# Casts of h in one chain in the down projection, and an earlier split of a sum of x in a SwiGLU block kernel

## The chip, the core and the metric

The kernel runs on one core of a Trainium2 chip. The metric is the device time of one execution in microseconds (us). Of several executions the median is given. A profiled execution is one more, from which the page and the trace come.

TensorE (PE in the profile) multiplies matrices into PSUM banks, VectorE (DVE) and ScalarE (ACT) do the elementwise work, GpSimd (POOL) and SyncE (SP) mostly issue DMAs here.

## The reference

One layer of an encoder on 512 tokens of width 1024, all in float32:

```python
for l in range(DEPTH):                                   # DEPTH = 1
    x = x + FFN_RES * _swiglu(_rmsnorm(x, norm_ffn1[l]), w_ffn1_gu[l], w_ffn1_down[l])
    h = _rmsnorm(x, norm_mix[l])
    ...                                                  # RG-LRU both ways, neighbourhood attention
    x = x + y @ w_out[l]
    x = x + FFN_RES * _swiglu(_rmsnorm(x, norm_ffn2[l]), w_ffn2_gu[l], w_ffn2_down[l])

def _swiglu(h, w_gu, w_down):
    g, u = jnp.split(h @ w_gu, 2, axis=-1)
    return (jax.nn.silu(g) * u) @ w_down
```

The change is in the two SwiGLU layers (FFN below). Their inner width, the features of h = silu(g) * u, is 2816: 22 tiles of 128 features.

## The kernel before

**Numbers.** Each float32 operand is split in a high part H, rounded to the type fp32r by a cast on ScalarE (L140, in `split`), and the remainder L, a subtraction on VectorE (L143) that needs the cast. A product is three matmuls: H by H, L by H, H by L. In names, `wh`/`wl` are the parts of weights, `xh`/`xl` of x, `hh`/`hl` of h, and `s1` to `s4` stand for sums of parts of x and both their parts.

**The products that give h.** Two of the 22 tiles of features are "plain". In the first FFN they are multiplied while x is loaded, kept token by token (`pre`), finished in `ready` (L508 to L511: silu, product, transpose, store to `hp`) and fetched back transposed. The other twenty are five units of four tiles, computed in `strassen` by a Strassen-Winograd scheme with seven products each, of the forms a11, a12, s1, s2, s4, s3, a22; a product is 24 matmuls (L317) into two banks. The sums of weights come from a DMA that accumulates on POOL's queue (`add`) and additions on VectorE (`sums`, L340). The sums of x are made once (`make_forms`: `raw` subtracts, `cut` splits); in the first unit of the first FFN `need("s1")` and so on puts the splits where the code stands. The last product of a unit, a22, is done within the next unit. Banks are copied out on ScalarE (`evict`, L348) or added on VectorE (`plus`, L353).

**From there to the down projection.** `gate` (L359) is silu on ScalarE, `put` multiplies by u (L370) and transposes 32x32 blocks (L372) on VectorE, and `flush` stores the four tiles of a unit to DRAM, `hd[u]`. `fetch(u)` reads a unit back with features on the partitions: two tiles `hT` of 256 tokens, each with four DMAs of POOL's queue. `cut(k)` splits the tile k of h from these two halves (casts of 256 tokens each) into `hh` and `hl` of 512 tokens, and `ahead(n)` calls it for all k below n and fetches a unit ahead.

**The down projection.** Its sum goes over k, the 22 tiles of h, into eight banks (m = 0 to 7, four of the pool `aux`, four of `acc`), so 24 matmuls for each k (`mm3`, L167 to L169). The first three k (`DFIRST`) are done in four groups of two banks:

```python
for g in range(4):
    outs = range(2 * g, 2 * g + 2)
    for m in outs:
        ps[m] = (aux_t, acc_t)[g % 2]()
    for k in first:
        for m in outs:
            put_in(m, k)
```

The last group's banks are those of the last unit's last product (`Z`); they come free when its silu has read them. `finish` is called between that product and its silu: it fetches the first unit, loads the weights of the first three k and splits h ahead, with high priority. `last_put` and `flush` of the last unit stand behind it.

**What sets the order.** A scheduler orders the instructions of each engine by their dependences, with those under `tc.high_priority()` first. `after(i, prev)` tells the scheduler to place `i` behind `prev`; it adds no semaphore, so it binds on the chip only through the order within a queue. `hold` does so behind the matmul marked last. Four pairs of buffers hold wh and wl, three the raw weights (`wraw`), four the `pair` tiles, five the tiles `PT`, which the loads of weights and `hT` share.

Of the kernel before, what the change touches and what calls it, by code (L numbers as in the profile page):

```python
# [86 lines left out]
def block_kernel(ctx: ExitStack, tc, a, out):  # L87
# [49 lines left out]

    def split(raw, H, L, act=True):
        if act:
            nc.scalar.activation(H, raw, AF.Copy)  # L140
        else:
            nc.vector.tensor_copy(H, raw)
        return nc.vector.tensor_tensor(L, raw, H.bitcast(F32), ALU.subtract)  # L143
# [96 lines left out]
    def after(i, prev, sync=False):  # L240

        i, prev = getattr(i, "ins", i), getattr(prev, "ins", prev)
        tc.add_manual_dep(i, prev.name, mybir.DependencyInfo(
            mybir.DependencyClass.Sync if sync else mybir.DependencyClass.NoSync, mybir.DependencyReason.DATA), reason="order")

    def hold(i):

        after(i, mark["mm"])
        return i
# [42 lines left out]
    def strassen(src, units, A, norm, hd, need, ready, finish, early):  # L292
# [58 lines left out]
        def plus(ts, pss):  # L351
            for t, ps in zip(ts, pss):
                nc.vector.tensor_tensor(t, t, ps, ALU.add)  # L353

        def gate(ts, th):
            ss = [big_t(n="s") for _ in ts]
            for tb, (s_, t) in enumerate(zip(ss, ts)):
                j = th * 2 + tb
                nc.scalar.activation(s_, t, AF.Silu, scale=rc[0][:, j : j + 1])  # L359
            return ss  # L360

        def flush(q=nc.sync):
            while out:
                to, t2 = out.pop(0)
                hold(q.dma_start(to, t2))

        def put(u, ss, ts, th):
            for tb, (s_, t) in enumerate(zip(ss, ts)):
                j = th * 2 + tb
                mark["h"] = nc.vector.scalar_tensor_tensor(t, t, rc[0][:, j : j + 1], s_, ALU.mult, ALU.mult)  # L370
                t2 = big_t(n="ht")
                nc.vector.transpose(  # L372
                    t2.rearrange("p (c f i) -> p f c i", c=NCB, i=32), t.rearrange("p (f c i) -> p f c i", c=NCB, i=32))
                out.append((hd[u][j], t2.rearrange("p (c x) -> p c x", c=NCB)))
# [1 line left out]
        def last_product(p, out_now=True):  # L376
            product(p["Z"], operands(p["a"]), "a22", False, True, out_now)

        def last_put(p):
            put(p["u"], gate(p["Z"], 1), p["u7"], 1)  # L380

        def begin(u):
            a_ = raws(u, 0, "pair", 4)
# [5 lines left out]
        for u in range(units):  # L389
            state_["u"] = u  # L390
            a_, Z, p1 = begun.pop(u) if u in begun else begin(u)
            c_ = raws(u, 2, "PT", 5)
            d_ = raws(u, 1, "PT", 5)
            b_ = raws(u, 3, "wraw", 3)
            if u == 0:
                add(u, a_, 1)
            if u == 0:
                rc.append(norm())
            if u == units - 1:
                need("plain")  # L400
            Y = [aux_t() for _ in range(2)]
            product(Y, operands(c_), "a12", True, True)
            if u == 0:
                need("s1")
            plus(p1, Y)
            if u > 0:
                s1 = gate(p1, 0)
            X = [aux_t() for _ in range(2)]
            w = operands(a_) if u == 0 else sums(a_, d_)
            product(X, w, "s1", True, False)  # L410
            add(u, d_, 3)
            p5 = evict(X, "p5")
            if u == 0 and early:
                begun[1] = begin(1)
            if prev:
                last_product(prev)
                last_put(prev)
            w = sums(a_, b_)
            if u == 0:
                need("s2")  # L420
            product(Z, w, "s2", False, False)
            add(u, a_, 2)
            u2 = evict(Z, "u2")
            if u == 0:
                need("s4")
            product(X, operands(b_), "s4", False, True)
            if u == 0:
                need("s3")
                ready(rc[0])
                s1 = gate(p1, 0)  # L430
            plus(u2, X)
            put(u, s1, u2, 0)
            product(Z, operands(d_), "s3", False, False, u < units - 1)
            plus(p5, Z)
            prev = dict(u=u, Z=Z, u7=p5, a=a_)
        last_product(prev, False)
        finish()
        last_put(prev)
        flush(nc.gpsimd)

    def ffn(wgu, ws, wd, xh, xl, forms, ssum, plain, res, emit_out, lead=None, end=None):
        units = (FT - plain) // 4
# [58 lines left out]
        def ready(rc):  # L501
            if not toks:
                return
            neg = tiny.tile([P, NCB], F32, tag="nrc", name=nm("nrc"))
            nc.vector.tensor_scalar(neg, rc, -1.0, None, ALU.mult)
            for tb, t in enumerate(toks):
                g, u = t[:, :half], t[:, half:]
                nc.scalar.activation(g, g, AF.Silu, scale=rc[:, tb : tb + 1])  # L508
                nc.vector.scalar_tensor_tensor(u, u, neg[:, tb : tb + 1], g, ALU.mult, ALU.mult)
                nc.vector.transpose(  # L510
                    g.rearrange("p (c f i) -> p f c i", c=NCB, i=32), u.rearrange("p (f c i) -> p f c i", c=NCB, i=32))  # L511
                hold(nc.sync.dma_start(hp[tb], g.rearrange("p (c x) -> p c x", c=NCB)))
# [3 lines left out]
             "a22": quarter(4, slice(half, T))}  # L516
        A.update({n: forms.S[n] for n in FORMS})

        turned, cuts = {}, {}

        def fetch(u):
            for th in range(2):
                t = big.tile([P, 8, NCB, 32], F32, tag="PT", bufs=5, name=nm("hT"))
                for c in range(NCB):
                    hold(nc.gpsimd.dma_start(
                        t[c * 32 : (c + 1) * 32].rearrange("p g f i -> p g (f i)"),
                        hd[u].rearrange("t (a i) c x -> c i (t a) x", a=NCB)[c][:, th * 8 : th * 8 + 8]))
                turned[u, th] = t
# [10 lines left out]
        def cut(k):  # L539
            cuts[k] = H, L = big_t(F32R, n="hh"), big_t(F32R, n="hl")  # L540
            if k < len(hs):
                split(hs[k], H, L)
                return
            u, f = (-1, k) if k < plain else divmod(k - plain, NCB)
            for th in range(2):
                c = slice(th * half, (th + 1) * half)
                v = lambda t: t[:, c].rearrange("p (g i) -> p g i", i=32)
                split(turned[u, th][:, :, f], v(H), v(L))

        def ahead(n):  # L550
            while len(cuts) < min(n, FT):
                k = len(cuts)
                if k >= plain and (k - plain) % NCB == 0:
                    u = (k - plain) // NCB
                    if u + 1 < units:
                        fetch(u + 1)
                cut(k)
# [5 lines left out]
        def finish():  # L563
            fetch(0)
            for k in first:
                ws_[k] = load_w(wd[k], 1024)
            with tc.high_priority():
                ahead(DFIRST + 3)

        strassen(ws, units, A, norm, hd, need, ready, finish, lead is not None)  # L570

# [704 lines left out]
```

## Time and profile before

| what | value |
|---|---|
| median of 3 runs | 1114.53 us (1113.95 to 1115.28) |
| the profiled execution | 1115.2 us |
| its span, first to last instruction | 1113.4 us |
| mean granted clock of TensorE | 0.99 |
| busy: TensorE, VectorE, ScalarE, POOL | 98, 69, 50, 18% |
| DMA | 198.17 MB, mean 178 GB/s |

In the rows of the profile that follow, a row of the order in time starts with the time from the span's start and the duration of one instruction in us, then the engine, the line of the kernel, the operation, the tiles written and read, and in brackets the wait just before and what ended it. A row of a stretch (A:B) has the length and then, for TensorE, its weight loads, VectorE, ScalarE and POOL, the busy us and the count; at its end the granted clock of TensorE (1.00 is full), the share of the DMA engines and GB/s. A row "out <- engine tile line" of the waits has us, count and the longest.

### The profile page before, as it was taken

The numbers are of one execution on the slowest core, as the hardware profiler recorded it, in microseconds if no ns is written. First come the engines' busy times: TensorE is split into PE (matmuls) and PEld (weight loads), VectorE is DVE, ScalarE is ACT, GpSimd is POOL, SyncE is SP. The second block draws the span as 40 slices with busy tenths as digits, with TensorE's granted clock in tenths as the row PEclk, the third lists the DMA queues.
The fourth block names the chain that finished last, engine by engine and source line by source line (L and its number), as shares of the span: only waits on it lengthen the run. The fifth ranks groups of instructions, "written<-read, shape, count | busy, mean of one in ns | idle before, by whom it ended". The sixth has DMA issues, their size and how long they took to land. (4 is left out here: it accounts for less than half of the span.)

```text
span 1113.4 us, 14401 instructions
## 1 busy us (share of the span) xinstructions
PE 1086.3 (98%) x5121; PEld 888.7 (80%) x5121; DVE 770.7 (69%) x1222; ACT 562.0 (50%) x866; POOL 197.7 (18%) x340
## 2 busy tenths in 40 slices
PE   9989999969999999999999999999999999989998
PEld 7778888858888777888877788888888888868887
DVE  6778788773325786899878896768677788772322
ACT  7745555542324668776645543356455555543310
POOL 0101012432000243132226322000001000331000
PEclk9999999999999999999999999999999999999999
DMA  9777766884332578384679566565476767774222
GB/s 362 167 193 191 204 177 161 213 250 128 101 102 90 165 209 232 121 234 119 198 222 257 163 220 219 154 229 176 99 194 180 193 195 170 200 245 140 95 76 76
DMA packets 67463, 198.17 MB, mean 178 GB/s; under 512 B 11072, under 2 KB 12864, under 8 KB 67392
## 3 DMA queue, kind: packets, MB, share of 16 engines
q1 hardware_dynamic: 46592, 136.60, 37.3%
q0 software_dynamic: 20512, 60.34, 24.2%
q8 instruction: 40, 0.66, 0.2%
q10 hardware_dynamic: 288, 0.32, 0.1%
q14 instruction: 31, 0.25, 0.1%
HBM read 162.06 MB, written 26.74 MB: 170 GB/s over the span
## 5 line engine op out<-in xcount | busy, mean ns | idle before, releaser
L143 DVE TENSOR_TENSOR wl<-wraw,wh 128x1024 fp32r<-128x1024 f32 (+2 forms) x147 | 168.7, 1149 | 173.4 <-ACT wh L140 170.5
L140 ACT ACTIVATE wh<-wraw 128x1024 fp32r<-128x1024 f32 (+2 forms) x135 | 134.5, 998 | 239.2 <-PE acc L168 163.7
L143 DVE TENSOR_TENSOR wl<-pair,wh 128x1024 fp32r<-128x1024 f32 x80 | 97.2, 1219 | 46.0 <-ACT wh L140 45.8
L140 ACT ACTIVATE wh<-pair 128x1024 fp32r<-128x1024 f32 x80 | 84.8, 1061 | 72.1 <-PE aux L317 51.9
L167 PE MATMUL acc<-xh,wh 128*128 128x512 f32 x288 | 113.9, 395 | 0.0
L169 PE MATMUL acc<-xh,wl 128*128 128x512 f32 x288 | 112.5, 391 | 0.0
L168 PE MATMUL acc<-xl,wh 128*128 128x512 f32 x288 | 112.5, 391 | 0.0
L317 PE MATMUL acc<-wh,s 128*128 128x512 f32 x320 | 99.1, 390 | 3.1 <-ACT s L140 2.0
L317 PE MATMUL aux<-wh,s 128*128 128x512 f32 x320 | 100.0, 393 | 2.1 <-ACT s L140 2.0
L167 PE MATMUL aux<-hh,wh 128*128 128x512 f32 (+1 forms) x179 | 70.4, 395 | 8.5 <-ACT hh L140 8.5
L168 PE MATMUL aux<-hl,wh 128*128 128x512 f32 (+1 forms) x179 | 70.7, 395 | 5.4 <-DVE hl L143 5.2
L892 PE MATMUL acc<-wh,xh 128*128 128x512 f32 x192 | 75.7, 394 | 0.0
L893 PE MATMUL acc<-wh,xl 128*128 128x512 f32 x192 | 74.8, 389 | 0.0
L894 PE MATMUL acc<-wl,xh 128*128 128x512 f32 x192 | 74.7, 389 | 0.0
L317 PEld LDWEIGHTS acc<-wh,s 128*128 128x128 f32 x320 | 60.0, 188 | 16.7 <-ACT s L140 2.4
L317 PEld LDWEIGHTS aux<-wh,s 128*128 128x128 f32 x320 | 60.7, 190 | 15.6 <-ACT s L140 2.4
L169 PE MATMUL aux<-hh,wl 128*128 128x512 f32 (+1 forms) x179 | 70.3, 393 | 0.0
L168 PE MATMUL acc<-hl,wh 128*128 128x512 f32 (+1 forms) x176 | 69.0, 392 | 0.0
L167 PE MATMUL acc<-hh,wh 128*128 128x512 f32 (+1 forms) x176 | 69.0, 393 | 0.0
L169 PE MATMUL acc<-hh,wl 128*128 128x512 f32 (+1 forms) x176 | 68.9, 391 | 0.0
L140 ACT ACTIVATE wh<-PT 128x1024 fp32r<-128x1024 f32 x40 | 42.3, 1060 | 44.9 <-PE acc L317 35.8
L167 PEld LDWEIGHTS acc<-xh,wh 128*128 128x128 f32 x288 | 54.1, 188 | 13.0 <-issue 2.3
(230 smaller groups left out, 2431.8 us busy)
## 6 DMA issues: line engine op xcount, KB each, us to landing
wraw<-wqkv SPq DMA_DIRECT2D x24, 512.0 KB, 4.3
wraw<-wg SPq DMA_DIRECT2D x24, 512.0 KB, 7.3
wraw<-w1d SPq DMA_DIRECT2D x22, 512.0 KB, 5.0
wraw<-w2d SPq DMA_DIRECT2D x22, 512.0 KB, 3.3
PT<-w1s SPq DMA_DIRECT2D x20, 512.0 KB, 6.1
hT<-hd POOLq DMA_DIRECT2D x80, 128.0 KB, 5.2
PT<-w2s SPq DMA_DIRECT2D x20, 512.0 KB, 4.0
hd<-ht SPq DMA_DIRECT2D x32, 256.0 KB, 6.1
```

Source lines behind the costliest of these rows:

```text
L140: nc.scalar.activation(H, raw, AF.Copy)
L143: return nc.vector.tensor_tensor(L, raw, H.bitcast(F32), ALU.subtract)
L167: nc.tensor.matmul(ps, wh, xh, start=first, stop=False, skip_group_check=skip)
L168: nc.tensor.matmul(ps, wh, xl, start=False, stop=False, skip_group_check=skip)
L169: mark["mm"] = nc.tensor.matmul(ps, wl, xh, start=False, stop=last, skip_group_check=skip)
L317: mark["mm"] = nc.tensor.matmul(pss[tb], x_[:, s], w_[:, c], start=first and k == 0 and x_ is xh_ and w_ is H, stop=k == 3 and w_ is L, sk ...
L892: nc.tensor.matmul(pss[j], xh[kk][:, tj], H[:, s], start=kk == 0, stop=False)
L893: nc.tensor.matmul(pss[j], xl[kk][:, tj], H[:, s], start=False, stop=False)
L894: mark["mm"] = nc.tensor.matmul(pss[j], xh[kk][:, tj], L[:, s], start=False, stop=kk == KT - 1)
```

## The change

In both down projections the casts of h are chained, each after the one that was made before it (`cast`), so that the two halves of a tile follow each other. `finish` splits four tiles ahead instead of six and without high priority, and fetches two units there (`fetch(1)` was called within `ahead`, at the first tile of the first unit, before; hence `k > plain`). The last silu (`gate` in `last_put`) is ordered behind the latest cast, which is that of the tile k = 3, and the last stores behind the last fetch. In the first unit of the first FFN `need("s2")` stands right behind `need("s1")` instead of behind the sums of weights of s2, and the first multiplication on a plain column block (L509 before, L512 after) is ordered behind the split of s4.

```diff
@@ -137,7 +137,7 @@
 
     def split(raw, H, L, act=True):
         if act:
-            nc.scalar.activation(H, raw, AF.Copy)
+            mark["H"] = nc.scalar.activation(H, raw, AF.Copy)
         else:
             nc.vector.tensor_copy(H, raw)
         return nc.vector.tensor_tensor(L, raw, H.bitcast(F32), ALU.subtract)
@@ -352,17 +352,21 @@
             for t, ps in zip(ts, pss):
                 nc.vector.tensor_tensor(t, t, ps, ALU.add)
 
-        def gate(ts, th):
+        def gate(ts, th, prev=None):
             ss = [big_t(n="s") for _ in ts]
             for tb, (s_, t) in enumerate(zip(ss, ts)):
                 j = th * 2 + tb
-                nc.scalar.activation(s_, t, AF.Silu, scale=rc[0][:, j : j + 1])
+                i = nc.scalar.activation(s_, t, AF.Silu, scale=rc[0][:, j : j + 1])
+                if prev is not None:
+                    after(i, prev)
             return ss
 
-        def flush(q=nc.sync):
+        def flush(q=nc.sync, prev=None):
             while out:
                 to, t2 = out.pop(0)
-                hold(q.dma_start(to, t2))
+                i = hold(q.dma_start(to, t2))
+                if prev is not None:
+                    after(i, prev)
 
         def put(u, ss, ts, th):
             for tb, (s_, t) in enumerate(zip(ss, ts)):
@@ -376,8 +380,8 @@
         def last_product(p, out_now=True):
             product(p["Z"], operands(p["a"]), "a22", False, True, out_now)
 
-        def last_put(p):
-            put(p["u"], gate(p["Z"], 1), p["u7"], 1)
+        def last_put(p, prev=None):
+            put(p["u"], gate(p["Z"], 1, prev), p["u7"], 1)
 
         def begin(u):
             a_ = raws(u, 0, "pair", 4)
@@ -402,6 +406,7 @@
             product(Y, operands(c_), "a12", True, True)
             if u == 0:
                 need("s1")
+                need("s2")
             plus(p1, Y)
             if u > 0:
                 s1 = gate(p1, 0)
@@ -416,8 +421,6 @@
                 last_product(prev)
                 last_put(prev)
             w = sums(a_, b_)
-            if u == 0:
-                need("s2")
             product(Z, w, "s2", False, False)
             add(u, a_, 2)
             u2 = evict(Z, "u2")
@@ -435,8 +438,8 @@
             prev = dict(u=u, Z=Z, u7=p5, a=a_)
         last_product(prev, False)
         finish()
-        last_put(prev)
-        flush(nc.gpsimd)
+        last_put(prev, mark["H"])
+        flush(nc.gpsimd, mark["fetch"])
 
     def ffn(wgu, ws, wd, xh, xl, forms, ssum, plain, res, emit_out, lead=None, end=None):
         units = (FT - plain) // 4
@@ -506,7 +509,7 @@
             for tb, t in enumerate(toks):
                 g, u = t[:, :half], t[:, half:]
                 nc.scalar.activation(g, g, AF.Silu, scale=rc[:, tb : tb + 1])
-                nc.vector.scalar_tensor_tensor(u, u, neg[:, tb : tb + 1], g, ALU.mult, ALU.mult)
+                after(nc.vector.scalar_tensor_tensor(u, u, neg[:, tb : tb + 1], g, ALU.mult, ALU.mult), mark["cut", "s4"])
                 nc.vector.transpose(
                     g.rearrange("p (c f i) -> p f c i", c=NCB, i=32), u.rearrange("p (f c i) -> p f c i", c=NCB, i=32))
                 hold(nc.sync.dma_start(hp[tb], g.rearrange("p (c x) -> p c x", c=NCB)))
@@ -516,13 +519,13 @@
              "a22": quarter(4, slice(half, T))}
         A.update({n: forms.S[n] for n in FORMS})
 
-        turned, cuts = {}, {}
+        turned, cuts, cast = {}, {}, []
 
         def fetch(u):
             for th in range(2):
                 t = big.tile([P, 8, NCB, 32], F32, tag="PT", bufs=5, name=nm("hT"))
                 for c in range(NCB):
-                    hold(nc.gpsimd.dma_start(
+                    mark["fetch"] = hold(nc.gpsimd.dma_start(
                         t[c * 32 : (c + 1) * 32].rearrange("p g f i -> p g (f i)"),
                         hd[u].rearrange("t (a i) c x -> c i (t a) x", a=NCB)[c][:, th * 8 : th * 8 + 8]))
                 turned[u, th] = t
@@ -545,12 +548,16 @@
             for th in range(2):
                 c = slice(th * half, (th + 1) * half)
                 v = lambda t: t[:, c].rearrange("p (g i) -> p g i", i=32)
+                prev = cast[-1:]
                 split(turned[u, th][:, :, f], v(H), v(L))
+                if prev:
+                    after(mark["H"], prev[0])
+                cast.append(mark["H"])
 
         def ahead(n):
             while len(cuts) < min(n, FT):
                 k = len(cuts)
-                if k >= plain and (k - plain) % NCB == 0:
+                if k > plain and (k - plain) % NCB == 0:
                     u = (k - plain) // NCB
                     if u + 1 < units:
                         fetch(u + 1)
@@ -564,8 +571,8 @@
             fetch(0)
             for k in first:
                 ws_[k] = load_w(wd[k], 1024)
-            with tc.high_priority():
-                ahead(DFIRST + 3)
+            fetch(1)
+            ahead(DFIRST + 1)
 
         strassen(ws, units, A, norm, hd, need, ready, finish, lead is not None)
```

The order of ScalarE at the end of the first `strassen`. `wraw` here is a weight of the down projection; `hT_391` and `hT_392` are the first and second 256 tokens of the first unit, and `hh_408`, `hh_410` the tiles k = 2 and 3. Before:

```order
L140 ACTIVATE wh_429_2082<-wraw_428_2081 128x1024
L140 ACTIVATE hh_408_1963<-hT_391_1913 128x256
L140 ACTIVATE hh_410_1969<-hT_391_1913 128x256
L140 ACTIVATE hh_412_1975<-hT_391_1913 128x256
L140 ACTIVATE hh_414_1981<-hT_391_1913 128x256
L359 ACTIVATE s_416_1987<-acc_331_1581,rcol_107_428 128x512
L359 ACTIVATE s_417_1988<-acc_332_1582,rcol_107_428 128x512
L140 ACTIVATE wh_438_2134<-wraw_437_2133 128x1024
L720 ACT_TABLE_LOAD
...
L140 ACTIVATE hh_408_1963<-hT_392_1918 128x256
L140 ACTIVATE hh_410_1969<-hT_392_1918 128x256
```

and after:

```order
L140 ACTIVATE wh_425_2070<-wraw_424_2069 128x1024
L140 ACTIVATE hh_408_1963<-hT_391_1913 128x256
L140 ACTIVATE hh_408_1963<-hT_392_1918 128x256
L140 ACTIVATE hh_410_1969<-hT_391_1913 128x256
L140 ACTIVATE hh_410_1969<-hT_392_1918 128x256
L359 ACTIVATE s_412_1975<-acc_331_1581,rcol_107_428 128x512
L359 ACTIVATE s_413_1976<-acc_332_1582,rcol_107_428 128x512
L140 ACTIVATE hh_427_2075<-hT_391_1913 128x256
L140 ACTIVATE hh_427_2075<-hT_392_1918 128x256
L140 ACTIVATE hh_429_2081<-hT_391_1913 128x256
L140 ACTIVATE hh_429_2081<-hT_392_1918 128x256
L727 ACT_TABLE_LOAD
```

The four casts ahead of the silu (L359) are now both halves of k = 2 and k = 3, and were the first halves of k = 2 to 5.

The order of TensorE in the first groups of the first down projection. The tiles `hh_402` and `hh_404` are k = 0 and 1 before (`hh_404` and `hh_406` after), `hh_408` is k = 2; the banks of the first, third and last group are aux_420, aux_424 and acc_426 before, aux_416, aux_420 and acc_422 after. Before:

```order
L167 MATMUL aux_425_2042<-hh_404_1947,wh_397_1930 128x512
L168 MATMUL aux_425_2042<-hl_405_1948,wh_397_1930 128x512
L169 MATMUL aux_425_2042<-hh_404_1947,wl_398_1931 128x512
L167 MATMUL acc_426_2061<-hh_402_1941,wh_394_1924 128x512
L168 MATMUL acc_426_2061<-hl_403_1942,wh_394_1924 128x512
L169 MATMUL acc_426_2061<-hh_402_1941,wl_395_1925 128x512
...
L167 MATMUL acc_427_2062<-hh_404_1947,wh_397_1930 128x512
L168 MATMUL acc_427_2062<-hl_405_1948,wh_397_1930 128x512
L169 MATMUL acc_427_2062<-hh_404_1947,wl_398_1931 128x512
L167 MATMUL aux_420_2001<-hh_408_1963,wh_400_1936 128x512
L168 MATMUL aux_420_2001<-hl_409_1964,wh_400_1936 128x512
```

and after:

```order
L167 MATMUL aux_421_2030<-hh_406_1957,wh_397_1930 128x512
L168 MATMUL aux_421_2030<-hl_407_1958,wh_397_1930 128x512
L169 MATMUL aux_421_2030<-hh_406_1957,wl_398_1931 128x512
L167 MATMUL aux_416_1989<-hh_408_1963,wh_400_1936 128x512
L168 MATMUL aux_416_1989<-hl_409_1964,wh_400_1936 128x512
L169 MATMUL aux_416_1989<-hh_408_1963,wl_401_1937 128x512
...
L167 MATMUL aux_421_2030<-hh_408_1963,wh_400_1936 128x512
L168 MATMUL aux_421_2030<-hl_409_1964,wh_400_1936 128x512
L169 MATMUL aux_421_2030<-hh_408_1963,wl_401_1937 128x512
L167 MATMUL acc_422_2049<-hh_404_1951,wh_394_1924 128x512
L168 MATMUL acc_422_2049<-hl_405_1952,wh_394_1924 128x512
```

The last pair of banks now has its first matmul behind k = 2 of the other three pairs, where k = 2 stood behind k = 0 and 1 of all four.

The order of VectorE at the end of the first unit of the first FFN. `wl_180` is the remainder of the second unit's next weights, `u2` and `p5` the sums of the first unit that are finished here. Before:

```order
L258 TENSOR_TENSOR s3_156_651<-xg_50_175 128x256
L143 TENSOR_TENSOR wl_180_746<-PT_171_731,wh_179_745 128x1024
L143 TENSOR_TENSOR s3_158_655<-s3_156_651,s3_157_654 128x512
L258 TENSOR_TENSOR s3_159_658<-xg_55_201 128x256
L258 TENSOR_TENSOR s3_159_658<-xg_60_227 128x256
L353 TENSOR_TENSOR u2_144_601<-u2_144_601,aux_118_475 128x512
L353 TENSOR_TENSOR u2_145_602<-u2_145_602,aux_119_476 128x512
L143 TENSOR_TENSOR s3_161_662<-s3_159_658,s3_160_661 128x512
L143 TENSOR_TENSOR wl_182_762<-PT_172_733,wh_181_761 128x1024
L370 SCALAR_TENSOR_TENSOR u2_144_601<-u2_144_601,rcol_107_428,s_163_683 128x512
L370 SCALAR_TENSOR_TENSOR u2_145_602<-u2_145_602,rcol_107_428,s_164_684 128x512
L372 STREAM_TRANSPOSE ht_165_690<-u2_144_601 128x4x4x32
```

and after:

```order
L143 TENSOR_TENSOR s3_161_662<-s3_159_658,s3_160_661 128x512
L513 STREAM_TRANSPOSE pre_88_363<-pre_88_363 128x2x4x32
L353 TENSOR_TENSOR u2_144_601<-u2_144_601,aux_122_483 128x512
L353 TENSOR_TENSOR u2_145_602<-u2_145_602,aux_123_484 128x512
L374 SCALAR_TENSOR_TENSOR u2_144_601<-u2_144_601,rcol_107_428,s_163_683 128x512
L374 SCALAR_TENSOR_TENSOR u2_145_602<-u2_145_602,rcol_107_428,s_164_684 128x512
L376 STREAM_TRANSPOSE ht_165_690<-u2_144_601 128x4x4x32
L376 STREAM_TRANSPOSE ht_166_693<-u2_145_602 128x4x4x32
L353 TENSOR_TENSOR p5_128_519<-p5_128_519,acc_91_369 128x512
L353 TENSOR_TENSOR p5_129_520<-p5_129_520,acc_92_370 128x512
L143 TENSOR_TENSOR wl_180_746<-PT_171_731,wh_179_745 128x1024
L143 TENSOR_TENSOR wl_182_762<-PT_172_733,wh_181_761 128x1024
```

The remainder `wl_180` stood ahead of the second half of s3 and now stands behind the whole finish of the unit, and transposes of the plain columns (`pre`) have come in between.

## The prediction, made before the changed kernel was run

> **What bounds the kernel now.** I read, in this order: the busy times of the page; the waits of TensorE; busy times and granted clock in stretches of 10 us and finer; then the instructions in order of time around the three places that these point to.
>
> ```profile
> PE 1086.3 (98%) x5121; PEld 888.7 (80%) x5121; DVE 770.7 (69%) x1222; ACT 562.0 (50%) x866; POOL 197.7 (18%) x340
> ...
> PE aux L167 <- ACT hh L140: 8.5, 2, 4.8
> PE aux L168 <- DVE hl L143: 5.2, 2, 4.5
> PE acc L317 <- ACT s L140: 2.0, 1, 2.0
> PE aux L317 <- ACT s L140: 2.0, 1, 2.0
> ...
> 240.00:250.00 10.00, 1.41 (x4) 0.44 (x3) 8.86 (x34) 6.31 (x16) 6.67 (x12) 0.78 0.90 251
> 990.00:1000.00 10.00, 5.60 (x21) 4.00 (x20) 6.59 (x15) 5.79 (x14) 7.94 (x14) 0.83 0.78 238
> ...
> 46.99 0.39 PE L317 MATMUL acc<-wh,xh 128*128 128x512 f32 x1
> 52.21 0.39 PE L317 MATMUL acc<-wl,xh 128*128 128x512 f32 x1
> ```
>
> TensorE is the bound nearly everywhere. It is idle for only 27 us of the span (1113.4), and 13.7 us of that are waits for hh and hl, the two parts of h, twice each: at the starts of the two down projections. 4 us more are waits for casts of the sums s of x. In the stretches the first pair after the width is TensorE's busy time and count; the last three numbers are the granted clock, the share of the DMA engines and GB/s. The clock is low where the gaps are, so a gap costs more than its length. The last two rows are the first and last of 24 matmuls without a wait: 0.227 us each at full clock. I call the places B (240 us), C (990 us) and A (50 to 80 us, the first unit of the first FFN).
>
> **B, the first down projection.**
>
> ```profile
> 223.75 0.62 PE L167 MATMUL aux<-hh,wh 128*128 128x512 f32 x2
> 225.50 0.40 PE L317 MATMUL acc<-wh,xh 128*128 128x512 f32 x1
> 232.41 1.06 ACT L140 ACTIVATE wh<-wraw 128x1024 fp32r<-128x1024 f32 x1 [1.97 <-DMA wraw<-w1d]
> 233.38 1.32 ACT L140 ACTIVATE hh<-hT 128x256 fp32r<-128x256 f32 x4
> 234.61 1.24 ACT L359 ACTIVATE s<-acc,rcol 128x512 f32<-128x512 f32 x2
> 234.65 1.42 DVE L143 TENSOR_TENSOR hl<-hT,hh 128x256 fp32r<-128x256 f32 x4
> 240.29 0.39 PE L169 MATMUL acc<-hh,wl 128*128 128x512 f32 x1
> 242.57 3.77 ACT L140 ACTIVATE hh<-hT 128x256 fp32r<-128x256 f32 x12
> 248.91 2.77 DVE L143 TENSOR_TENSOR hl<-hT,hh 128x256 fp32r<-128x256 f32 x8
> 250.73 0.80 PE L168 MATMUL aux<-hl,wh 128*128 128x512 f32 x1 [4.53 <-DVE hl L143]
> 258.46 0.39 PE L167 MATMUL aux<-hh,wh 128*128 128x512 f32 x1
> ...
> 219.34 0.58 POOL L525 DMA_DIRECT2D hT<-hd  x1 [0.86 <-DMA hT<-hd]
> ...
> DMA to landing us min/median/max: 2.5/5.3/9.4
> ```
>
> A matmul needs all 512 tokens of h, so both halves of a tile. At 233.38 ScalarE casts four first halves (tiles k = 2 to 5). Their second halves are in the group of twelve at 242.57, behind two weight casts that wait for TensorE; VectorE takes their remainders at 248.91, behind a polynomial. So TensorE ends its 72 matmuls of the last product and of k = 0 and 1 at 240.5, has k = 2 complete only at 250.73, takes 7.7 us for its other 23 matmuls (5.2 at full clock), and starts k = 3 at 258.46.
>
> The change pairs the halves: the four casts at 233.38 become both halves of k = 2 and of k = 3, instructions of the same kind at the same place, and the two silu still follow. The remainder of k = 2 is then there after two of the four subtractions, near 235.4. The PE rows also put k = 2 of the first three pairs of banks ahead of the last pair. From 223.75 I count three matmuls of k = 0, then the 24 of the last product. These wait for the additions that read their banks, which now stand together on VectorE: 0.4 us, as much as is lost there before (225.50 is the seventh matmul from 223.75). k = 2 is reached 60 matmuls after 223.75, at 223.75 + 13.6 + 0.4 = 237.8, later than 235.4: no wait. The last pair of banks is reached 18 matmuls later, at 241.8, and silu, which frees it, ends at 235.85. All 96 matmuls take 21.8 + 0.4, and k = 3 starts at 245.9 instead of 258.46: **12.5 us**.
>
> What else moves here I cost at nothing, with these covers. The weights of k = 4 need a buffer that k = 0 holds until its last matmul, the 83rd, ends at 243.1; cast (1.06) and remainder (about 1.2) end near 245.5, and TensorE wants them after k = 3, at 251.3. If that cover went, each us beyond it would be a us lost. The remainders of k = 4 and 5 now stand ahead of the polynomial, whose results no matmul of the down projection uses. On POOL's queue three fetches of the first unit pass the eight of the second; all sixteen were issued by 220 and no fetch took over 9.4 us, so the order among them is covered by the cast at 233.38, and so are the stores behind them. A bound from below: if the weights of k = 3 (cast at 232.41, after a wait of 1.97) came later by twice that wait, k = 2 would be 1.5 us late. From above: the 0.4 us also go. B gives 11.0 to 12.9.
>
> **C, the second down projection.**
>
> ```profile
> 984.95 1.32 ACT L140 ACTIVATE hh<-hT 128x256 fp32r<-128x256 f32 x4
> 993.53 0.39 PE L169 MATMUL acc<-hh,wl 128*128 128x512 f32 x1
> 997.60 0.79 PE L167 MATMUL aux<-hh,wh 128*128 128x512 f32 x1 [3.68 <-ACT hh L140]
> 999.11 0.80 PE L168 MATMUL aux<-hl,wh 128*128 128x512 f32 x1 [0.72 <-DVE hl L143]
> 1006.45 0.39 PE L167 MATMUL aux<-hh,wh 128*128 128x512 f32 x1
> ```
>
> The same change of order. The matmul at 993.53 is the 72nd; k = 2's 24 follow without a wait, and k = 3 starts at 993.76 + 24 x 0.227 = 999.2 instead of 1006.45: **7.3 us**. k = 2 is now wanted 14 matmuls before 993.76, near 990.5, and is ready two casts and, behind a weight's remainder, two subtractions after 984.95, near 987. The margin is wider than in B and no transfer is waited for; I keep 7.1 to 7.4.
>
> **A, the first unit.**
>
> ```profile
> 54.55 0.73 PE L317 MATMUL acc<-wh,s 128*128 128x512 f32 x2 [1.96 <-ACT s L140]
> 63.65 1.54 PE L317 MATMUL aux<-wh,s 128*128 128x512 f32 x3 [1.96 <-ACT s L140]
> 78.68 0.39 PE L317 MATMUL aux<-wl,xh 128*128 128x512 f32 x1
> ...
> 50.00:60.00 10.00, 6.92 (x30) 5.09 (x29) 7.08 (x12) 4.88 (x7) 1.71 (x2) 1.00 0.97 193
> 60.00:70.00 10.00, 7.92 (x27) 5.75 (x26) 7.08 (x12) 4.67 (x7) 0.88 (x1) 0.83 0.71 194
> 62.00:64.00 2.00, 0.35 (x2) 0.30 (x2) 1.37 (x2) 1.60 (x3) 0.00 (x0) 1.00 0.96 309
> ...
> 61.13 0.33 SPq L301 DMA_DIRECT2D PT<-w1s  x1
> 65.04 1.22 DVE L340 TENSOR_TENSOR pair<-pair,PT 128x1024 f32<-128x1024 f32 x1
> 72.01 1.27 DVE L353 TENSOR_TENSOR u<-u,aux 128x512 f32<-128x512 f32 x2
> 74.95 1.41 DVE L370 SCALAR_TENSOR_TENSOR u<-u,rcol,s 128x512 f32<-128x512 f32 x2
> 76.27 1.30 DVE L372 STREAM_TRANSPOSE ht<-u 128x512 f32<-128x512 f32 x2
> 77.49 1.24 DVE L353 TENSOR_TENSOR p<-p,acc 128x512 f32<-128x512 f32 x2
> ```
>
> Splitting s2 early takes away the gap before 54.55 and one just behind it: its product can start at 52.44 and end at 57.9 instead of 61.7 (63.65 less 1.96), 3.8 us earlier. Most of that is given back, in three places.
> - The gap before 63.65 stays: the casts of s4 still stand on ScalarE behind two weight casts and the two copies out of the banks of s2. Its product starts near 60.1, a gap of 2.2 us.
> - The addition at 65.04 needs a weight load that SyncE issued at 61.13 and that now goes out near 57.5, when its buffer is free. The DMA engines are full then (share 0.96), with as many bytes ahead of it as before. Bounds: 3.9 us after issue, the most that it took before, so 61.4; or no earlier than before, at most 65.0. I take 64.0, nearer the latter because the engines are full. The second half of s4 then waits, and goes on at 65.8: a gap of 2.4 us.
> - On VectorE the remainder wl of the second unit's next weights now stands behind the whole finish of the first unit (the last four rows). From the last remainder of s3 VectorE has a transpose of the plain columns (0.4), then 1.27 + 1.41 + 1.30 + 1.24 and the remainder itself, 1.2: with overlaps 6.5 us. TensorE needs 19 matmuls, 4.3 us, for the same way. This new gap is 2.1 us and ends at 77.7.
>
> TensorE stood at that matmul, the eighth of the next product and on, at 78.68 before. **A gives 1.0 us**; with the load there at 61.4 it gives 3.3. The steps on the plain columns that the diff pins behind the s4 remainder (L509 and L510 of the profile), and on SyncE their stores and the loads that slip behind these, serve products that TensorE reaches over 30 us later.
>
> In the stretch from 60 us, with one gap of 1.96 us, the clock is 0.83 on the mean: 1.7 us of ten are lost. From 50 us, with a gap as long, it is 1.00. So a gap of 2 us can cost 1.7 us more, and need not. A lies between -1.7 and 3.3. The Trainium skill (TensorE: Matmul & The Clock Gate, HAM oscillation) warns only of idle gaps over about 3.4 us; by that rule none of A's gaps would touch the clock, and the sum is the one below. The trace disagrees in the stretch from 60 us.
>
> **Sum.** The profiled execution took 1115.2 us: its span, 1113.4, and 1.8 around it. 1115.2 - 12.5 - 7.3 - 1.0 = 1094.4. The median of the runs, 1114.53, lies 0.7 lower, less than one drop of the clock in A; I do not correct for it.
>
> **Rivals.**
> - The clock drops after one or two of A's gaps where it would not have before: 1096.1 to 1097.8. For and against it stand the two stretches in A.
> - Another wait takes half of B: ScalarE is one queue, and the four casts stand behind the weight cast that waited for its transfer (232.41). The margin at k = 2 is 2.4 us; a transfer that ended 8.7 us later would cost 6.3 us and give 1100.7. Against it: the change adds no transfer, so nothing new competes with it.
> - Slower than before: silu now stands by rule behind the fourth cast, so a late second half holds the casts, silu, the last banks and every weight cast behind them. It decides from the point where the fetches land, in both places, after the four casts' time by 12.5 + 2.4 us (B) and as long in C: 1117 and up. In B that is after 248, and the last fetch, issued at 219.34, can be there by 229.
> - The change does not do what it says, and the chip still has halves of k = 2 apart: only A is left, 1114.2. The order of the built program speaks against it.
>
> **Chances.** As summed 0.62 (own range 1092 to 1097); clock 0.20; half of B lost 0.12; slower 0.03; no change (within 0.2%, 2.2 us, the least that a measurement here tells apart) 0.02; other ways of faster 0.01. Range: from 1091.5 (12.9 + 7.4 + 3.3 off) to 1099.5 (11.0 + 7.1 - 1.7 off gives 1098.8, and part of the third case). Faster 0.95, the same 0.02, slower 0.03.
>
> **What would show it.** B and C: no wait of TensorE for hh or hl, clock 1.00 from 230 to 270 us, four casts and then silu on ScalarE. A: no gap at 52; gaps for s4's cast, for its second half, and for wl behind the finish of the first unit. I am wrong if TensorE waits for hh or hl in the new order, or for the weights of k = 3 to 6, or if A is off by more than 3 us.

## The result, and the profile after

The changed kernel takes 1095.66 us (median of 4 runs, 1094.92 to 1097.02), the kernel before 1114.24 (4 runs, 1113.24 to 1115.28): a ratio of 0.9835 with a 95% interval of 0.9818 to 0.9852. The forecast was 1094.4. The profiled execution took 1095.27, its span 1093.5, 19.9 us less than that of before.

From the page after and its waits of TensorE (us in total, times, longest), the lines that answer to those of before:

```profile
PE 1079.7 (99%) x5121; PEld 885.9 (81%) x5121; DVE 771.2 (71%) x1222; ACT 561.9 (51%) x866; POOL 198.0 (18%) x340
...
PE aux L317 <- ACT s L140: 2.0, 1, 2.0
PE aux L1018 <- DVE kl L997: 1.9, 1, 1.9
PE aux L1081 <- DVE ql L994: 1.7, 1, 1.7
PE aux L317 <- DVE wl L143: 1.4, 1, 1.4
PE aux L317 <- DVE s L143: 1.1, 1, 1.1
...
240.00:250.00 10.00, 10.00 (x46) 8.27 (x45) 8.23 (x25) 6.39 (x11) 3.87 (x8) 1.00 0.79 249
970.00:980.00 10.00, 10.00 (x46) 8.29 (x45) 7.20 (x15) 4.97 (x12) 2.99 (x6) 1.00 0.50 168
980.00:990.00 10.00, 10.00 (x46) 8.29 (x45) 5.10 (x8) 5.33 (x10) 5.05 (x9) 1.00 0.76 229
```

The waits for hh and hl, 13.7 us of TensorE's idle time, are gone. Both starts of a down projection run at 46 matmuls in 10 us at full clock. What is left are gaps of 0.8 to 2.0 us, the longest of them in the first unit and in the attention (`kl`, `ql`).

Where the 19.9 us are is read from casts on ScalarE that stand at the same step in both profiles. Rows in order of time, before:

```profile
28.33 1.09 ACT L470 ACTIVATE pre<-aux 128x512 f32<-128x512 f32 x2 [5.65 <-PE aux L467]
95.88 1.07 ACT L140 ACTIVATE wh<-PT 128x1024 fp32r<-128x1024 f32 x1 [0.96 <-PE acc L317]
258.48 1.06 ACT L140 ACTIVATE wh<-wraw 128x1024 fp32r<-128x1024 f32 x1 [12.14 <-issue]
731.21 1.06 ACT L140 ACTIVATE wh<-wraw 128x1024 fp32r<-128x1024 f32 x1 [1.31 <-PE acc L168]
963.65 1.06 ACT L140 ACTIVATE wh<-PT 128x1024 fp32r<-128x1024 f32 x1 [0.96 <-PE acc L317]
1006.42 1.06 ACT L140 ACTIVATE wh<-wraw 128x1024 fp32r<-128x1024 f32 x1 [7.96 <-PE acc L168]
```

and after:

```profile
26.11 1.09 ACT L473 ACTIVATE pre<-aux 128x512 f32<-128x512 f32 x2 [3.57 <-PE aux L470]
92.98 1.06 ACT L140 ACTIVATE wh<-PT 128x1024 fp32r<-128x1024 f32 x1 [0.96 <-PE acc L317]
242.99 1.06 ACT L140 ACTIVATE wh<-wraw 128x1024 fp32r<-128x1024 f32 x1 [0.30 <-PE acc L168]
718.31 1.06 ACT L140 ACTIVATE wh<-wraw 128x1024 fp32r<-128x1024 f32 x1 [1.31 <-PE acc L168]
950.77 1.07 ACT L140 ACTIVATE wh<-PT 128x1024 fp32r<-128x1024 f32 x1 [0.96 <-PE acc L317]
986.26 1.06 ACT L140 ACTIVATE wh<-wraw 128x1024 fp32r<-128x1024 f32 x1 [0.30 <-PE acc L168]
```

The differences, row by row, are 2.22, 2.90, 15.49, 12.90, 12.88 and 20.16 us. So the start (before any step of the change) gives 2.2, A 0.7, B 12.6, C 7.3; the mixer (RG-LRU and attention, between the FFNs) takes 2.6 back, and 0.3 go at the end (20.16 to 19.9). The same sum for every kernel of this study, in us earlier than the profile of before (in B medians over the rest of that down projection, so the last digit can differ by 0.1), with the median of its runs. One execution of the kernel with two edits at A took 1351.04 us at a granted clock of 0.752 and is left out of its median. The ratios below are each against executions of the kernel before from the same round: their median was 1114.42 us for the chain alone, four ahead with low priority and the two kernels that part A from the rest, 1115.73 for the two delays and the two sets of edits at A, and 1114.60 for the other two. Medians from different rounds can be compared only to about that 1.5 us.

| kernel | start | A | B | mixer | C | median us |
|---|---|---|---|---|---|---|
| changed | 2.2 | 0.7 | 12.6 | -2.6 | 7.3 | 1095.66 |
| chain alone | -0.1 | -1.1 | 12.5 | -1.8 | 7.3 | 1097.02 |
| four ahead, low priority | 0.1 | -1.1 | 7.9 | -0.6 | 4.3 | 1102.59 |
| six ahead, low priority | 2.1 | -1.0 | 10.7 | 0.9 | 5.4 | 1098.86 |
| four ahead, high priority | 0.1 | 0.0 | -0.4 | 0.9 | -0.6 | 1115.95 |
| changed, without its part on A | 2.1 | -0.9 | 12.6 | 0.7 | 7.3 | 1095.67 |
| its part on A alone | 2.1 | 0.7 | -0.2 | -0.2 | -0.1 | 1114.76 |
| changed, short delay | 0.1 | 0.2 | 12.6 | -2.2 | 7.3 | 1093.83 |
| changed, long delay | 2.2 | -1.9 | 4.4 | -0.8 | 1.1 | 1109.76 |
| changed, two edits at A | 2.3 | 1.8 | 12.6 | -0.8 | 7.3 | 1094.64 |
| changed, three edits at A | 0.5 | 7.2 | 12.6 | -1.9 | 7.3 | 1089.46 |

B and C repeat to 0.1 us where the order is the same and k = 2 is there in time. Start, A and mixer do not.

### The profile page after: what moved, and what is told of

The parts are those of the page before. It is cut to its first block, busy times and chain, and to the rows that moved or that the text cites. A ratio compares the mean times of both kernels' runs of the same rounds, so it can differ in the third digit from the quotient of the medians.

```text
span 1093.5 us, 14407 instructions
## 1 busy us (share of the span) xinstructions
PE 1079.7 (99%) x5121; PEld 885.9 (81%) x5121; DVE 771.2 (71%) x1222; ACT 561.9 (51%) x866; POOL 198.0 (18%) x340
## 4 chain that ended last, share of the span: by engine, by line
PE 89%; DVE 2%; DMA 1%; ACT 1%; issue 0%; ACTq 0%; DVEq 0%
PE acc L317 18%; PE aux L317 13%; PE acc L167 10%; PE acc L168 10%; PE acc L169 10%; PE acc L899 4%; PE acc L900 4%; PE acc L901 4%; PE aux L169 4%; PE aux L168 4%; PE aux L167 4%; PE aux L1081 1%; PE aux L810 1%; DMA vd<-v 1%; PE aux L1018 1%; DVE wl L143 1%
## 5 line engine op out<-in xcount | busy, mean ns | idle before, releaser
L317 PEld LDWEIGHTS acc<-wh,s 128*128 128x128 f32 x320 | 60.1, 188 | 12.5
```

Of the source, the lines that this page charges most:

```text
L317: mark["mm"] = nc.tensor.matmul(pss[tb], x_[:, s], w_[:, c], start=first and k == 0 and x_ is xh_ and w_ is H, stop=k == 3 and w_ is L, sk ...
```

## Experiments on the down projections

**The chain alone.** The kernel before, and only:

```diff
                 v = lambda t: t[:, c].rearrange("p (g i) -> p g i", i=32)
+                prev = cast[-1:]
                 split(turned[u, th][:, :, f], v(H), v(L))
+                if prev:
+                    after(mark["H"], prev[0])
+                cast.append(mark["H"])
```

> The kernel before, with one thing of the change: the casts of h in one chain. Six tiles are still split ahead with high priority, so eight half casts and not four stand ahead of the last silu, and fetches, stores and the first unit are as before. Pairing theory (both halves of k = 2 must be through ScalarE and VectorE before TensorE has done k = 0 and 1): k = 2 is complete as early as in the changed kernel, the silu ends 1.3 us later than there, within the 7 us that its banks have to spare, so the gain of both down projections is there in full: 12.5 + 7.3, a time near 1095 (1093 to 1097), and no wait of TensorE for hh or hl. Rival (the gain needs the silu behind only four casts, or the second unit's fetches ahead of the last stores): half of it at the most, 1104 or more, with a wait at the last two banks or for hT of the second unit.

Measured: 1097.02, at the upper edge of its range, ratio 0.9839 (0.9822 to 0.9856), B and C in full, and no wait for hh or hl. ScalarE in B:

```profile
234.28 2.55 ACT L140 ACTIVATE hh<-hT 128x256 fp32r<-128x256 f32 x8
236.74 1.24 ACT L359 ACTIVATE s<-acc,rcol 128x512 f32<-128x512 f32 x2
```

Eight half casts stand ahead of the silu and nothing is lost by that. So the pairing of the halves is enough. The silu behind the fourth cast, the fetches ahead and the stores behind them add nothing that can be seen.

**Number and priority of the tiles split ahead.** Three kernels without a chain, silu and stores as before:

```diff
-            with tc.high_priority():
-                ahead(DFIRST + 3)
+            ahead(DFIRST + 1)
```

> The kernel before, with another thing of the change alone: four tiles split ahead instead of six, without high priority; no chain, silu, stores and fetches as before. Only the first halves of k = 2 and 3 then stand ahead of the silu, and the second halves still behind two weight casts that wait for TensorE. Pairing theory: no gain, 1114 (1112 to 1117), with the same two waits for hh and hl at each start of a down projection. Rival (fewer casts ahead of the silu is what helps): 1104 or less.

Measured: 1102.59, ratio 0.9887 (0.9866 to 0.9907), 7.9 + 4.3 us. That was a miss: I had made two weight casts that wait for TensorE the whole delay. The second pair of runs parts number and priority: `ahead(DFIRST + 3)` without high priority, and `ahead(DFIRST + 1)` with it.

> The kernel before, with six tiles split ahead as there but without high priority; no chain. The second half of k = 2 then stands right behind the two weight casts that wait for TensorE, as with four tiles ahead, and no longer behind the second unit's eight half casts. If the priority is what gave four tiles ahead its part: as that kernel, 7.9 + 4.3 = 12.2 us in the two down projections, 1102.5 (1100 to 1105), with a wait of about 1.5 us for hh and 1 us for hl at each. If the number of tiles did: no gain, 1114.5.

> The kernel before, with four tiles split ahead but with high priority as there; no chain. The second half of k = 2 then stands behind two weight casts, two first halves and the second unit's eight half casts. If the priority is what counts: as before, 1114.5 (1112 to 1117), since the second half comes 10 casts of 0.33 us behind the weight casts. If the number of tiles does: 1102.5.

Measured: six ahead with low priority 1098.86, below its range, ratio 0.9855 (0.983 to 0.9879); four ahead with high priority 1115.95, ratio 1.001 (0.9998 to 1.0022). It is the priority. With it the second unit's eight half casts go ahead of the second half of k = 2, as in the group of twelve at 242.57 in the profile of before. In both, TensorE goes on with k = 2 when about nine casts of that group are done, 2.9 us after its start. The waits of TensorE in the kernel with four ahead and high priority and its group of twelve, then the waits at B with six and with four ahead at low priority:

```profile
PE aux L167 <- ACT hh L140: 10.0, 2, 6.1
PE aux L168 <- DVE hl L143: 5.1, 2, 4.0
...
243.60 3.78 ACT L140 ACTIVATE hh<-hT 128x256 fp32r<-128x256 f32 x12
246.52 0.79 PE L167 MATMUL aux<-hh,wh 128*128 128x512 f32 x1 [6.06 <-ACT hh L140]
```

```profile
240.68 0.73 PE L167 MATMUL aux<-hh,wh 128*128 128x512 f32 x2 [1.23 <-ACT hh L140]
```

```profile
243.19 0.73 PE L167 MATMUL aux<-hh,wh 128*128 128x512 f32 x2 [1.53 <-ACT hh L140]
244.93 0.50 PE L168 MATMUL aux<-hl,wh 128*128 128x512 f32 x1 [1.00 <-DVE hl L143]
...
246.00:248.00 2.00, 2.00 (x6) 1.60 (x5) 1.62 (x10) 0.21 (x1) 1.91 (x5) 0.50 0.88 342
```

With low priority only the two weight casts are in the way: 1.9 us (12.6 - 10.7) with six ahead, for a wait of 1.23 us at full clock; why a wait costs 0.7 us more than its idle time there is open. With four ahead there are a second gap and a stretch at half clock behind it, 4.7 us in all. I had expected the two to be alike; that they differ by 2.8 us in B is about the second gap and 1.7 us of clock.

**How much the place bears.** In the changed kernel, n more casts ahead of the first half of k = 2, in both down projections (8 and 22; an addition to ScalarE's work, nothing reads the tile):

```diff
+                if (u, f, th) == (0, 0, 0):
+                    for j in range(n):
+                        i = nc.scalar.activation(
+                            spare, spare if j else turned[u, th].rearrange("p g f i -> p (g f i)")[:, :half], AF.Copy, scale=1.0 + j / 64)
+                        if prev:
+                            after(i, prev[0])
+                        prev = [i]
```

> The changed kernel with 8 more casts of 256 elements on ScalarE (into a tile that nothing reads) ahead of the first cast of k = 2 in both down projections: about 8 x 0.33 = 2.7 us, up to 3.4 if each waits for the one before it. In the changed kernel the remainder of k = 2 is ready 3.5 us ahead of its first matmul in B (231.3 against 234.8) and 4.3 us ahead in C. Pairing theory with that margin: nothing is lost, 1095.7 (1094 to 1097.5), no wait of TensorE for hh or hl. Rival (ScalarE's queue is the path there, so that each us on it costs one): 2 x 2.7 = 5.4 us more, 1101.

> The same with 22 casts: about 7.3 us (to 9.5). Pairing theory: TensorE waits for k = 2 at both places, 7.3 - 3.5 = 3.8 us in B and 7.3 - 4.3 = 3.0 in C (to 6.0 and 5.2), and behind each gap the clock drops for one or two stretches of 3.4 us, 1.7 us lost in each: 10 us more (8 to 18), near 1106. The silu is late by as much, but its banks have 7.1 us to spare plus the gap. If gaps cost only their length: 1102.5. Rival (the delay costs in full at both places): 14.6 us more, 1110, with a wait at the last banks.

Measured: 1093.83, ratio 0.9814 (0.9794 to 0.9833), for the short delay, 0.2 below its range, and 1109.76, ratio 0.9955 (0.9941 to 0.997), for the long one. Rows of the short delay, then of the long one:

```profile
233.05 3.12 ACT L555 ACTIVATE spare<-spare 128x256 f32<-128x256 f32 x7
236.07 1.32 ACT L141 ACTIVATE hh<-hT 128x256 fp32r<-128x256 f32 x4
```

```profile
PE aux L168 <- ACT hh L141: 9.9, 2, 5.8
...
233.35 9.39 ACT L555 ACTIVATE spare<-spare 128x256 f32<-128x256 f32 x21
243.41 0.79 PE L168 MATMUL aux<-hh,wh 128*128 128x512 f32 x1 [5.85 <-ACT hh L141]
...
242.00:246.00 4.00, 2.59 (x6) 2.01 (x7) 2.85 (x7) 3.97 (x12) 0.00 (x0) 0.50 0.00 0
```

Each cast waits for the one before it and takes 0.45 us, so the delays are 3.5 and 9.7 us. The short one costs nothing in B or C: it fits the margin of 3.5 us. The long one gives waits of 5.85 us in B and 4.0 in C (9.9 in all) against 6.2 and 5.4 by the margins, and B and C lose 8.2 and 6.2. The rest, 2.4 and 2.1 us, is mostly the clock behind the gap, 0.50 from 242 to 246 us. So a late k = 2 costs its gap and about 2 us more, and an early one gains nothing. The time of the long delay lies nearer to the rival's 1110 than to the 1106 of the pairing theory, because the casts took 0.45 us and not 0.33; what speaks against the rival are the waits, which are shorter than the delay of 9.7 us by 3.9 and 5.7, and that no wait for the last banks is there. (The waits end with the casts of k = 2, and these had 4.8 us to spare in B and 5.6 in C in the changed kernel; in B a weight's load came 1.0 us later too. So 5.9 and 4.1 would be right where the margins of the remainders give 6.2 and 5.4.)

## Experiments on the first unit

> The changed kernel without its part on the first unit: the second sum of x is split where it was, and the plain column step is not ordered behind the split of s4. Theory: the places B and C keep their 12.6 and 7.3 us; only A is lost, so TensorE is 0.7 us (0 to 1.5) behind the changed kernel from the second unit on: near 1096.3. Rival (the early split of s2 is what brings part of the 20 us): 2 us or more behind the changed kernel.

> The kernel before, with the change's part on the first unit alone: the second sum of x split with the first, and the plain column step behind the split of s4. Theory: 0.7 us less than before (-1 to 2.5 less, the width being one drop of the clock in A), that is 1113.5, with three gaps at A: for the cast of s4, for the remainder of s4 behind an addition that waits for its load, and for the weights' remainder behind the first unit's finish. Rival: the 3.8 us of the gap at s2 are gained in full, 1110.5.

The edit, put alone into the kernel before in the second run and taken out of the changed kernel in the first:

```diff
             if u == 0:
                 need("s1")
+                need("s2")
...
-            if u == 0:
-                need("s2")
             product(Z, w, "s2", False, False)
...
-                nc.vector.scalar_tensor_tensor(u, u, neg[:, tb : tb + 1], g, ALU.mult, ALU.mult)
+                after(nc.vector.scalar_tensor_tensor(u, u, neg[:, tb : tb + 1], g, ALU.mult, ALU.mult), mark["cut", "s4"])
```

Measured: 1095.67, ratio 0.9828 (0.9811 to 0.9845), without the part on A, and 1114.76, ratio 0.9996 (0.9985 to 1.0006), with it alone. By the times the part on A can't be told from nothing. By the profiles A is 0.7, 0.7, 0.2 and -1.9 us where it is changed (the four kernels of the table that have just this part) and 0, -1.1, -1.1, -1.0, -0.9 and 0.0 where it is as before. With one drop of the clock at A the changed part is 0.2 to 0.7 us ahead; with two drops it has -1.9 against about -1.0. So a gain of this part is not shown.

A in the changed kernel, with the stretch from 60 us:

```profile
57.77 1.35 PE L317 MATMUL aux<-wh,s 128*128 128x512 f32 x3 [1.96 <-ACT s L140]
62.25 1.22 DVE L340 TENSOR_TENSOR pair<-pair,PT 128x1024 f32<-128x1024 f32 x1 [3.01 <-DMA PT<-w1s]
64.13 0.50 PE L317 MATMUL aux<-wh,s 128*128 128x512 f32 x1 [1.13 <-DVE s L143]
75.61 0.74 PE L317 MATMUL aux<-wl,xh 128*128 128x512 f32 x2 [1.44 <-DVE wl L143]
...
60.00:70.00 10.00, 8.87 (x34) 6.82 (x33) 7.75 (x17) 4.91 (x7) 0.88 (x1) 0.86 0.68 195
```

These are the three gaps of the forecast, and they name three edits: the weights' addition behind the split of s4, the next weights' split with high priority, and s4 split ahead of the product of s2.

```diff
-            with nullcontext() if state_["u"] < 2 and early else tc.high_priority():
+            with nullcontext() if state_["u"] < 1 and early else tc.high_priority():
                 split(raw, *w)
...
-                    nc.vector.tensor_tensor(t, t, o, ALU.add)
+                    i = nc.vector.tensor_tensor(t, t, o, ALU.add)
+                    if early and state_["u"] == 1:
+                        after(i, mark["cut", "s4"])
...
+            if u == 0:
+                need("s4")
             product(Z, w, "s2", False, False)
             add(u, a_, 2)
             u2 = evict(Z, "u2")
-            if u == 0:
-                need("s4")
```

> The changed kernel with two edits at A: the additions of the second unit's weights are ordered behind the split of s4, and the second unit's first weights are split with high priority, so that their remainder stands on VectorE ahead of the first unit's finish. Theory: the gap behind the late load (1.13 us) and the one for wl (1.44) go, the one for the cast of s4 (1.96) stays: 2.6 us less than the changed kernel, 1093.1 (1091.4 to 1095.5; 1.7 either way is one drop of the clock). Rival: another wait takes their place, since the additions then stand behind the finish (pair for the next product): no change, 1095.7.

> The same, and s4 is subtracted and split ahead of the product of s2, so that its cast stands ahead of the copies out of the banks. Theory: all three gaps at A go, 1.96 + 1.13 + 1.44 = 4.5 us, and with them the drop of the clock behind the first (1.7 us): 4.5 to 6.2 us less than the changed kernel, 1089.5 to 1091.2. Rival: VectorE, which is full from 43 to 52 us, takes as much ahead of the product of s2 as it gives back: 1094 or more with a new gap before or within that product.

Measured: with the first two edits 1094.64, ratio 0.9815 (0.9792 to 0.9837), A 1.8 us; with all three 1089.46, ratio 0.9769 (0.9755 to 0.9783), A 7.2 us. The first two bring 1.1 us in the profile and not the 2.6 expected: the wait for the cast of s4 stays, and new ones of 0.75 and 0.18 us for weight casts come at 77.25 and 80.82, so the rival came true in part. With all three, the stretches and the one wait that is left:

```profile
50.00:60.00 10.00, 10.00 (x46) 8.29 (x45) 9.60 (x17) 8.25 (x12) 0.86 (x1) 1.00 0.98 243
60.00:70.00 10.00, 10.00 (x46) 8.29 (x45) 10.00 (x17) 4.05 (x6) 0.00 (x0) 1.00 0.50 169
...
75.41 0.74 PE L317 MATMUL aux<-wl,s 128*128 128x512 f32 x2 [0.50 <-DVE wl L143]
```

TensorE is busy from 50 to 70 us at full clock. That is 6.5 us more than the changed kernel has at A, 4.0 of gaps (4.53 less 0.50) and most of the rest the drop of the clock that no longer comes. By the medians it is 6.2 us faster than the changed kernel, by the ratios (0.9769 against 0.9835) 7.4, the best version of this study.

## Why the prediction was right, point by point

- **B, 12.5 us: 12.6.** k = 3 starts at 242.96 in the profile after, 15.5 earlier than 258.46; 2.9 of that are older. The order is the one forecast:

```profile
228.37 1.06 ACT L140 ACTIVATE wh<-wraw 128x1024 fp32r<-128x1024 f32 x1 [2.74 <-DMA wraw<-w1d]
229.34 1.32 ACT L140 ACTIVATE hh<-hT 128x256 fp32r<-128x256 f32 x4
230.56 1.25 ACT L359 ACTIVATE s<-acc,rcol 128x512 f32<-128x512 f32 x2
230.61 1.43 DVE L143 TENSOR_TENSOR hl<-hT,hh 128x256 fp32r<-128x256 f32 x4
234.80 0.39 PE L167 MATMUL aux<-hh,wh 128*128 128x512 f32 x1
242.96 0.39 PE L167 MATMUL aux<-hh,wh 128*128 128x512 f32 x1
```

  Half of the four subtractions at 230.61 complete k = 2 near 231.3, and TensorE wants it at 234.80: a margin of 3.5 us where the forecast had 2.4. The weight cast ahead waited for its load longer than before (2.74 against 1.97 us), but it started 4.0 us earlier (228.37 against 232.41), more than the 2.9 that TensorE was ahead. So the later transfer of the rival that would have taken half of B did not come.
- **C, 7.3 us: 7.3.**
- **A, 1.0 us: 0.7**, inside its width. Put on the time of before (2.22 later), the product of s4 starts at 60.0 (forecast 60.1), the addition at 64.5 (64.0), the second half at 66.35 (65.8), the matmul behind wl at 77.8 (77.7). The gaps were 1.96, 1.13 and 1.44 us where I had 2.2, 2.4 and 2.1: the first half of s4 ran at half clock, so TensorE came later to the load that it waited for. The clock fell once at A, as it did before. The sum had no drop behind the new gaps; that the one that came fell into time in which TensorE would have waited anyway is luck, and with it that A is so near to 1.0. In the profile of the long delay, which has the same instructions at A, the first half of s4 ran at full clock, the wait for its second half was longer, and the clock was at half from within that wait for two stretches (0.50 from 64 to 70 us), so that A is -1.9:

```profile
64.78 0.80 PE L318 MATMUL aux<-wh,s 128*128 128x512 f32 x1 [3.32 <-DVE s L144]
```

- **What the sum did not have**: 2.2 us at the start and -2.6 in the mixer. The first matmuls of the two profiles, before and after:

```profile
5.88 1.62 PE L465 MATMUL aux<-wh,xh 128*128 128x512 f32 x3 [1.04 <-ACT xh L191]
```

```profile
5.60 0.94 PE L468 MATMUL aux<-wh,xh 128*128 128x512 f32 x3 [0.78 <-DVE wh L459]
```

  Three equal matmuls take 1.62 us in one execution and 0.94 in the other. In the eleven profiles of the table the start is 2.1 to 2.3 us earlier in six and within 0.5 of before in five, kernels with and without the change in either group, so it belongs to the execution. In the mixer, 1.1 us go where a softmax on ScalarE waits behind a store of v; the other part is a drop of the clock behind the gap for `kl`. Both profiles have that gap (1.88 us before, 1.86 after), only the one after has the drop. The stretches, after and, 14.4 us later, before:

```profile
604.00:608.00 4.00, 4.00 (x34) 3.66 (x35) 3.10 (x14) 3.96 (x10) 0.56 (x1) 0.68 0.46 149
```

```profile
618.00:622.00 4.00, 3.64 (x37) 3.30 (x38) 3.35 (x14) 3.96 (x8) 0.34 (x1) 1.00 0.47 165
```

  The mixer's part runs from -2.6 to 0.9 over the eleven. That these two errors nearly cancel is luck. Without the start, the mixer and the 0.3 at the end, the three places give 1115.2 - 20.6 = 1094.6.
- **What was put down wrongly**: of the reasons why k = 2 was late before, the two weight casts are 1.9 us of 12.6 in B and of 7.3 in C. The rest is what stood ahead of k = 2 under high priority: in C the second unit's half casts and remainders, in B also the polynomial on VectorE. The wait for hl is 4.53 us in B and 0.72 in C, where no polynomial stands ahead of the remainder; that is 3.8 of the 5.3 us by which B exceeds C. No run parts the polynomial from the half casts in B. The forecast did not rest on the shares, the expectation for four tiles ahead did.

What stays open: why the store of v is waited for 1.1 us longer, and what moves the mixer from one execution to another beyond the clock.

## What to carry to other kernels

When a consumer needs both halves of a tile, order the producers by tile and not by half: the same casts in another order were worth 1.6% here (the chain alone). High priority for a whole look-ahead also raises the parts that are wanted last, and these then stand ahead of what is wanted next. Read a gap's price as at least its length plus the clock behind it, and trust a forecast of a few us only to the 2 us or so by which the start and the drops of the clock differ from one execution to the next.

## What was not expected of the hardware

The granted clock falls to 0.50 for stretches of 3.4 us (59.3 to 62.7 us at A after), 1.7 us lost in each. Each profile with a gap of 1.96 us at A has one or two such stretches there; the one without such a gap, with three edits at A, has none. The gap for `kl` in the mixer brought one after (1.86 us) and none before (1.88 us). With four tiles ahead at low priority, 1.53 us with 1.00 us close behind it brought one in B, and 1.53 with 0.92 none in C; 1.23 us, with six ahead, brought none. So it differs between executions of the same instructions. The Trainium skill (TensorE: Matmul & The Clock Gate, HAM oscillation) puts the danger at idle gaps over about 3.4 us. Here gaps of 1.86 to 1.96 us were enough, though not each time.
